# A two-layer transformer on one core: the modulation computed as visits of two k tiles, its columns read back through DRAM, and twenty of its parts placed outside the first MLP

## The chip, the cores and the metric

The kernel runs on one core of a Trainium2 chip. The metric is the device time of one execution in microseconds (us), as the median of several runs.

## The reference

Two transformer layers over 256 context and 512 latent tokens of width 1024: layer 0 with differential attention (8 heads), layer 1 with neighbourhood attention (16 heads, handled as 8 groups of two), each followed by a squared-ReLU MLP of width 4096. Both halves of a layer are modulated by vectors that depend on the conditioning inputs `c` (latent tokens) and `c_ctx` (context tokens) only:

```python
for i in range(DEPTH):
    mod_l = split(silu(c) @ w_mod[i] + b_mod[i], 6)        # w_mod[i] is 1024 x 6144
    mod_c = split(silu(c_ctx) @ w_mod[i] + b_mod[i], 6)
    x = x + mod_l[2] * mixer_i(rms_norm(x, norm1_g[i]) * (1 + mod_l[1]) + mod_l[0], ...)
    x = x + mod_l[5] * mlp(rms_norm(x, norm2_g[i]) * (1 + mod_l[4]) + mod_l[3])
    # the context tokens likewise with mod_c; after the last layer they are not needed
```

So per layer there are six sections of 1024 numbers for two streams: shift, scale and gate of the mixer (0, 1, 2) and of the MLP (3, 4, 5). All data is float32; most products are made of split operands in three passes.

## The kernel before, in words

The program runs in stages, each with its own partition of PSUM banks: a prologue with the first head (0 to 65 us), the first attention's heads (65 to 480), its out projection (to 544), the first MLP with its blend (to about 1115), the second attention's eight groups (to 1466), their projection, and the second MLP (from about 1506).

Activations lie transposed, model columns on the partitions. Shifts and scales are therefore wanted as columns: `mB` (shift) and `mA` ((1 + scale) times the norm's gain), 8 k tiles x 2 streams per section. The gates are wanted as rows and go to a DRAM tensor, `gates`, from which a broadcast load fetches them.

The modulation is cut in 48 chunks (`mod_chunk`, 24 a layer: six sections by four quarters of 256 columns). A chunk needs 1 MB of `w_mod`, loaded by SP into the tile M (L163), and does 8 matmuls in plain float32 (L263; 16 instructions in the trace), where the silu columns are the stationary operand and k tile kt writes to the 32 partitions of its quarter of the array, kt mod 4. The result in PSUM bank A is thus four partial sums on partitions 0, 32, 64 and 96 on. ScalarE copies them to a tile T (L266). A tail adds the four up with a matmul against the constant `sel`: for shift and scale as a column pair (L278, two matmuls of T's halves, then one or two small VectorE instructions, L285 to L289), for a gate as a row (L269, then a load of the bias, a VectorE add, L273, and a store, L274).

Where the chunks stand: eight (sections 0 and 1 of layer 0) in `first_head`; sixteen in the first attention; twenty-four, all of layer 1, in the first MLP, one at a call of `sideB`, which also steps the bias tables of the second attention.

The order of work around them: in both attentions PE, SP and POOL (`PINNED`) follow the order of the program, which the strings `START0`, `CYCLE0`, `END0`, `CYCLE1`, `LAST1`, `END1` write out by hand; `run` walks through a string. A word is a step: `Q0a` half a projection of the next head (L416), `S`, `T`, `V`, `U`, `O` the steps of the heads in flight (an apostrophe is an older head), `w` a weight load (SP, L130), `c` its split in a high and a low part, `x`, `X` loads and splits for the out projection, `P` a step of that; `m` begins a chunk and loads the next one's weights, `n` does its tail. In the second attention U is the transposition of normed queries and keys (L642 and L644 on PE, waiting for Y that VectorE makes in L431), T the transposition of the softmax's output (L695), V the sum over values (L710), which VectorE adds up in a tile T (L718). VectorE's and ScalarE's orders, and all orders in the MLPs, are the compiler's. The MLP's matmuls are L853 and L913, its last down part L994. `gated` in `project` (L766) multiplies by a gate row into a tile T.

## Time and profile before

| | |
|---|---|
| median of 3 runs | 1871.44 us (1870.74 to 1871.74) |
| profiled execution | 1864.46 us, span 1862.7 us |
| mean granted clock of TensorE | 0.983 |
| busy: PE, DVE, POOL, ACT | 1742.6, 1262.4, 1029.3, 948.0 us |
| DMA | 225.97 MB, of which 48 loads of 1 MB for the modulation |

PE is TensorE's matmuls, PEld its weight loads, DVE VectorE, ACT ScalarE, POOL GpSimd, SP the engine that issues most loads. A row of the timeline gives the start, the duration, the engine, the line, the operation with its output and inputs, and in brackets how long the engine was idle before it and what ended that. A matmul's end overlaps the next one's start, so what a piece of work holds of PE is read from start to start.

### The profile page before, as it was taken

To read this page: it belongs to the slowest core of one execution; us is meant where nothing else is said; L and a number is where in the kernel's file an instruction comes from. 1 tells how busy PE (TensorE), PEld (TensorE's weight loads), DVE (VectorE), ACT (ScalarE), POOL (GpSimd) and SP (SyncE) were. 2 spreads that over 40 slices of the span, in tenths; PEclk is the share of its full clock that TensorE was granted. 3 is DMA by queue.
4 is the path that set the end of the run, shared out by engine and by line. 5 is a ranking of instruction groups with operands and counts; after the bars stand their busy time and mean duration, and the time that the engine had idled before them with its cause. 6 is when DMAs were issued, how large, how long until landed. Compare 5 with 4: busy or idle time off the path is not lost.

```text
span 1862.7 us, 27761 instructions
## 1 busy us (share of the span) xinstructions
PE 1742.6 (94%) x10046; PEld 1523.8 (82%) x10046; DVE 1262.4 (68%) x2330; ACT 948.0 (51%) x2002; POOL 1029.3 (55%) x1002
## 2 busy tenths in 40 slices
PE   6989999996999999999999998999998989999988
PEld 5868888884789888888887987989897777878867
DVE  4587777786666465456466865777777557777785
ACT  4476667765344333233333345777776454445432
POOL 3755666653334555555555732444445547778873
PEclk9999999997999999999999998999999989999999
DMA  8122222224436646646643331122222424334432
GB/s 335 43 86 80 89 87 68 69 87 150 163 123 161 191 159 163 198 145 178 198 143 112 108 107 61 58 71 77 66 69 86 147 95 140 128 124 126 150 135 77
DMA packets 88554, 225.97 MB, mean 121 GB/s; under 512 B 9248, under 2 KB 24544, under 8 KB 82272
## 3 DMA queue, kind: packets, MB, share of 16 engines
q1 hardware_dynamic: 78928, 211.19, 35.0%
q10 hardware_dynamic: 9488, 13.00, 1.9%
q8 instruction: 79, 1.29, 0.3%
q14 instruction: 59, 0.48, 0.1%
HBM read 205.91 MB, written 18.25 MB: 120 GB/s over the span
## 4 chain that ended last, share of the span: by engine, by line
PE 66%; DVE 11%; ACT 7%; POOL 6%; issue 5%; DMA 4%; ACTq 0%; POOLq 0%; SPq 0%; DVEq 0%
PE PD L853 20%; PE PA L416 14%; PE PB L913 6%; PE PA L913 5%; POOL W L152 4%; PE PA L761 4%; PE PA L994 3%; PE PB L560 2%; PE PA L263 2%; DMA R<-in_w_dram 2%; PE PS L525 2%; PE PQ L406 1%; ACT W L146 1%; PE PS L664 1%; PE PB L710 1%
## 5 line engine op out<-in xcount | busy, mean ns | idle before, releaser
L152 POOL TENSOR_TENSOR W<-R,W 128x512 fp32r<-128x512 f32 x270 | 402.7, 1519 | 169.3 <-ACT W L146 163.5
L853 PE MATMUL PD<-Q,W 128*128 128x384 f32 (+2 forms) x1992 | 390.1, 346 | 9.2 <-DVE Q L340 5.6
L853 PEld LDWEIGHTS PD<-Q,W 128*128 128x128 f32 x1992 | 345.4, 189 | 40.4 <-issue 7.8
L146 ACT ACTIVATE W<-R 128x1024 fp32r<-128x1024 f32 (+1 forms) x165 | 168.1, 1022 | 195.6 <-DMA R<-in_w_dram 35.2
L152 POOL TENSOR_TENSOR W<-N,W 128x512 fp32r<-128x512 f32 x98 | 139.2, 1441 | 142.8 <-ACT W L146 142.4
L913 PE MATMUL PB<-W,H 128*128 128x512 f32 x738 | 190.8, 395 | 7.0 <-DVE Q L921 4.3
L913 PE MATMUL PA<-W,H 128*128 128x512 f32 x732 | 190.9, 396 | 4.5 <-DVE H L921 3.4
L416 PE MATMUL PA<-W,Q 128*128 128x384 f32 (+1 forms) x1008 | 175.8, 326 | 1.0 <-ACT H L454 1.0
L913 PEld LDWEIGHTS PB<-W,H 128*128 128x128 f32 x738 | 138.5, 189 | 39.5 <-DVE Q L921 5.2
L913 PEld LDWEIGHTS PA<-W,H 128*128 128x128 f32 x732 | 137.2, 190 | 37.2 <-DVE H L921 5.0
L302 POOL TENSOR_TENSOR SQ<-SQ,half 128x4 f32<-128x4 f32 (+1 forms) x96 | 93.8, 978 | 124.4 <-DVE SQ L429 123.5
L416 PEld LDWEIGHTS PA<-W,Q 128*128 128x128 f32 x1008 | 159.9, 192 | 1.2 <-ACT H L454 1.2
L146 ACT ACTIVATE W<-N 128x1024 fp32r<-128x1024 f32 x49 | 51.9, 1058 | 149.3 <-PE PA L913 66.4
L416 PE MATMUL PA<-WB,H 128*128 128x384 f32 x576 | 108.6, 340 | 0.8 <-DVE Q L477 0.8
L761 PE MATMUL PA<-W,H 128*128 128x512 f32 x384 | 97.6, 404 | 6.4 <-ACT H L752 4.4
L416 PEld LDWEIGHTS PA<-WB,H 128*128 128x128 f32 x576 | 98.7, 188 | 1.8 <-DVE Q L477 1.1
L871 DVE SCALAR_TENSOR_TENSOR H<-N,H 128x512 fp32r<-128x512 f32 (+1 forms) x57 | 70.8, 1244 | 41.9 <-ACT H L870 41.6
L853 PE MATMUL PD<-H,W 128*128 128x512 f32 (+1 forms) x408 | 94.7, 382 | 0.0
L761 PEld LDWEIGHTS PA<-W,H 128*128 128x128 f32 x384 | 72.3, 194 | 24.4 <-ACT H L752 4.8
L531 ACT ACTIVATE E<-PS,SA 128x768 f32<-128x768 f32 (+1 forms) x96 | 72.9, 760 | 35.2 <-DVE SA L530 31.6
L530 DVE TENSOR_REDUCE SA<-PS 128x1 f32<-128x768 f32 (+1 forms) x96 | 74.5, 776 | 20.8 <-ACT E L531 11.5
L676 POOL TENSOR_SCALAR E<-E,SA 128x256 f32<-128x256 f32 x64 | 59.5, 940 | 52.2 <-DVE SA L673 51.5
(258 smaller groups left out, 3564.0 us busy)
## 6 DMA issues: line engine op xcount, KB each, us to landing
R<-in_w_dram SPq DMA_DIRECT2D x121, 512.0 KB
M<-in_wmod_dram SPq DMA_DIRECT2D x48, 1024.0 KB
N<-in_w_dram SPq DMA_DIRECT2D x49, 512.0 KB
R<-in_wqa_dram SPq DMA_DIRECT2D x32, 384.0 KB
R<-in_wqb_dram SPq DMA_DIRECT2D x32, 384.0 KB
Y<-in_rpb_dram SPq DMA_DIRECT2D x48, 128.0 KB
bias<-Y SPq DMA_DIRECT2D x48, 128.0 KB
X<-bias SPq DMA_DIRECT2D x8, 768.0 KB
```

The source lines that it names most:

```text
L146: high = nc.scalar.activation(w[:, 0, :n], raw, AF.Copy)
L152: low = (eng or nc.gpsimd).tensor_sub(w[:, 1, o:e], raw[:, o:e], w[:, 0, o:e].bitcast(F32))
L302: nc.gpsimd.tensor_tensor(r, ss, self.half[:, :n], op=ALU.pow)
L416: nc.tensor.matmul(acc[:, :n], hT[kt][:, x, P * i:P * i + P], w[kt // 2][:, y, o:o + n], start=(kt == 0 and p == 0), stop=(kt == KT - 1 an ...
L530: nc.vector.tensor_reduce(mx, s, op=ALU.max, axis=AX, negate=True)
L531: nc.scalar.activation(e[:, m, :nk], s, AF.Exp, bias=mx[:, 0:1], accum_out=sm[:, m:m + 1])
L676: nc.gpsimd.tensor_scalar_mul(e[:, 1, o:o + 256], e[:, 1, o:o + 256], r[:, 1:2])
L761: nc.tensor.matmul(ps, oHL[h][:, x, c:c + P], w[h // 2][:, y, 512 * (h % 2):512 * (h % 2) + 512], start=(first and h == hs[0] and p == 0), ...
L853: nc.tensor.matmul(ps[:, at:at + b1 - b0], w[kt // 4][:, x, o:o + P], hT[kt][:, y, b0:b1], start=(kt == 0 and p == 0), stop=(kt == KT - 1 ...
L871: nc.vector.scalar_tensor_tensor(u[:, 1], src, 1.0, u[:, 0].bitcast(F32), op0=ALU.mult, op1=ALU.subtract)
L913: nc.tensor.matmul(ps, u[:, x, f, P * i:P * i + P], w[:, y, 512 * f:512 * f + 512], start=(f == 0 and p == 0), stop=(f == 1 and p == 2))
L994: nc.tensor.matmul(ps, hd[:, x, P * i - c0:P * i - c0 + P], w[f][:, y, 512 * n:512 * n + 512], start=(f == 0 and p == 0), stop=(f == len(h ...
```

## The change

A section of 1024 columns is now computed in four visits of two k tiles each (`mod_visit`), for all its four quarters: quarter q's partial sums go to partitions 32 q on. A visit has as many matmuls of the same shape as a chunk had. VectorE adds the visit's PSUM result to an accumulator tile MA (128x256), which a load has filled with the bias (`b_mod` on the two used rows of each quarter). After the fourth visit ScalarE's queue stores the four quarters' rows to a DRAM tensor `rows`; gates are later read from there as before from `gates`. For shifts and scales SP reads the rows back as columns ahead of the next visit, two DMAs of 128x8 single elements (one a stream), and one VectorE instruction makes `mB` or `mA` of all eight k tiles (`mod_set`). The copy by ScalarE, the column pairs and the row matmuls are gone, except in the first eight chunks, which stay as they were but for the place of the bias add.

The other forty chunks are now forty visits, in other places. Twenty (layer 0's sections 2 to 5 and layer 1's section 0) stand in the first attention, which had sixteen: five in START0, ten in the cycles, five in END0, where n is a visit that uses bank C. Four (layer 1's section 1) stay in the first MLP. Sixteen (layer 1's sections 2 to 5, `late`) stand in the second attention, two a group, their weights loaded as two halves of 512 KB into the tile C4 (the mask's) and a new pool M. The tag T has one buffer instead of two, and MA has two.

In the first MLP, PE's order before. The names are: PD, PA, PB the banks, Q and H activations, W weights; `x6` counts equal rows.

```order
L853 MATMUL PD_7522<-Q_6285,W_7467 128x384 x3
L853 MATMUL PD_7522<-Q_6286,W_7467 128x384 x3
L263 MATMUL PA_7573<-M_7448,silu 32x256 x8
L913 MATMUL PA_7613<-W_7605,H_7609 128x512 x6
L913 MATMUL PB_7622<-W_7605,H_7609 128x512 x6
L913 MATMUL PB_7648<-W_7641,H_7645 128x512 x6
L853 MATMUL PD_7714<-Q_6279,W_7704 128x384 x3
L853 MATMUL PD_7714<-Q_6280,W_7704 128x384 x3
L853 MATMUL PD_7714<-Q_6281,W_7704 128x384 x3
L278 MATMUL PA_7573<-sel,T_7582 128x2 x2
L853 MATMUL PD_7714<-Q_6282,W_7704 128x384
L913 MATMUL PA_7631<-W_7605,H_7609 128x512 x6
```

And at the same place in the changed kernel, behind its four visits:

```order
L851 MATMUL PD_7520<-Q_6293,W_7465 128x384 x3
L851 MATMUL PD_7520<-Q_6294,W_7465 128x384 x3
L911 MATMUL PA_7597<-W_7589,H_7593 128x512 x6
L911 MATMUL PB_7606<-W_7589,H_7593 128x512 x6
L911 MATMUL PA_7615<-W_7589,H_7593 128x512 x6
L911 MATMUL PB_7632<-W_7625,H_7629 128x512 x6
L851 MATMUL PD_7680<-Q_6287,W_7670 128x384 x3
L851 MATMUL PD_7680<-Q_6288,W_7670 128x384 x3
L851 MATMUL PD_7680<-Q_6289,W_7670 128x384 x2
L911 MATMUL PA_7641<-W_7625,H_7629 128x512 x6
L851 MATMUL PD_7680<-Q_6289,W_7670 128x384
L851 MATMUL PD_7680<-Q_6290,W_7670 128x384 x2
```

The chunk (L263) and its column pair (L278) are gone from between the MLP's matmuls (L853 and L913, now L851 and L911), whose own order has shifted a little.

In the second attention, PE before, from a half of the query projection (L416) to the transposition of queries and keys (L642, L644) at U4':

```order
L416 MATMUL PA_12265<-W_12053,Q_6716 128x256 x3
L416 MATMUL PA_12265<-W_12053,Q_6717 128x256 x3
L695 MATMUL PB_12280<-ident,E_12096 128x128 x4
L695 MATMUL PB_12287<-ident,E_12096 128x128 x4
L642 MATMUL PA_12294<-ident,Y_12164 128x128
L644 MATMUL PA_12294<-ident,Y_12164 128x128
```

And in the changed kernel (L416, L695, L642, L644 are now L414, L693, L640, L642):

```order
L414 MATMUL PA_11988<-W_11756,Q_6724 128x256 x3
L414 MATMUL PA_11988<-W_11756,Q_6725 128x256 x3
L289 MATMUL PA_12001<-C_11896,silu 32x256 x4
L289 MATMUL PA_12001<-M_11897,silu 32x256 x4
L693 MATMUL PB_12017<-ident,E_11799 128x128 x4
L693 MATMUL PB_12024<-ident,E_11799 128x128 x4
L640 MATMUL PA_12031<-ident,Y_11867 128x128
L642 MATMUL PA_12031<-ident,Y_11867 128x128
```

A visit (L289), four matmuls on each half of its weights, has come in ahead of L693. The second visit of a group stands likewise ahead of the L640 of U2.

On SP in the changed kernel, where a section has just been completed in the second attention (MA the bias, C and M the halves of a visit's weights, R weights of a later group, SA the columns read back, X a bias table):

```order
L1051 DMA MA_14054<-in_bmod_dram 128x256
L163 DMA C_14056<-in_wmod_dram 128x1024
L163 DMA M_14057<-in_wmod_dram 128x1024
L130 DMA R_14144<-in_wqb_dram 128x768
L130 DMA R_14146<-in_wqb_dram 128x768
L1060 DMA SA_14161<-rows 128x8x1 x2
L163 DMA C_14175<-in_wmod_dram 128x1024
L163 DMA M_14176<-in_wmod_dram 128x1024
L130 DMA R_14233<-in_wqb_dram 128x768
L130 DMA R_14465<-in_wqb_dram 128x768
L635 DMA X_14549<-bias 128x1536
```

And VectorE there (L291 the add of a visit, L279 the column set, L695 the eviction of the transposed softmax, before L697, L716 the sum over values, before L718, L429 the norm's product, before L431):

```order
L427 TENSOR_REDUCE SQ_14121<-sq_83 128x4
L451 TENSOR_TENSOR H_14002<-PA_14060,H_14001 64x256
L716 TENSOR_TENSOR T_13996<-PB_14131,T_13996 64x256
L291 TENSOR_TENSOR MA_14054<-PA_14165,MA_14054 128x256
L451 TENSOR_TENSOR H_14002<-PA_14060,H_14001 64x256
L695 TENSOR_TENSOR N_14179<-PB_14181,N_14179 128x512
L279 SCALAR_TENSOR_TENSOR mA<-SA_14161,gT 128x16
L695 TENSOR_TENSOR N_14180<-PB_14188,N_14180 128x512
L429 SCALAR_TENSOR_TENSOR Y_14118<-Y_14118,SQ_14123 128x256
```

The reads stand behind the next visit's two halves and two weights; the column set stands behind the next visit's add and between the two evictions of one T step.

The diff, cut: left out are the removed lines of `mod_chunk` and `Mods` (they stand in the listing above), the loads of `w_mod` by a shared helper `mod_raw` (SP, one 1 MB load or two halves), and the tables' new layouts.

```diff
--- before.py
+++ after.py
@@ -35,19 +35,19 @@
-CYCLE0 = """w0 w1 Q0a O2'' n1' S1' O3'' V4'' V5'' c0 w2 U4' Q0b c1 w3 Q1a T0' T1' Q1b c2 O4'' S2' V0' Q2a O5'' Q2b
-S3' T2' U0 Q3a V1' c3 O0' Q3b S4' T3' Q4a Q4b V2' O1' m0 S5' T4' U2 n0 Q5a V3' Q5b m1 S0 T5'"""
-START0 = """w0' w1' Q0a' Q0b' Q1a' U0'' Q1b' c0' w2' Q2a' Q2b' U2'' c1' w3' Q3a' Q3b' S0'' U4'' c2' Q4a' S1'' m0 c3'
-T0'' Q4b' S2'' V0'' n0 T1'' V1'' S3'' T2'' U0' Q5a' Q5b' m2 O0'' S4'' T3'' n2 w0 w1 Q0a U2' O1'' V2''
-S5'' T4'' Q0b c0 w2 V3'' S0' Q1a O2'' V4'' U4' Q1b c1 w3 O3'' T5'' m3 O4'' S1' T0' V5'' c2 V0' n3 S2' T1'
-Q2a O5'' Q2b S3' V1' c3 O0' U0 Q3a T2' Q3b Q4a S4' T3' Q4b V2' Q5a T4' S5' O1' V3' Q5b S0 T5' m1 U2"""
-END0 = """x0 x1 x2 x3 S1' O2'' O3'' V4'' T0' U4' n1' X0 V5'' T1' X1 S2' O4'' X2 x4 V0' S3' x5 P0a O5'' T2' X3 P1a
-X4 V1' O0' S4' X5 B0 P0b m0 V2' O1' x6 P1b T3' n0 P2a T4' S5' P2b O2' P3a V3' V4' P3b m1 T5' P4a O3' n1
+CYCLE0 = """w0 w1 Q0a O2'' S1' O3'' V4'' V5'' c0 w2 U4' Q0b c1 w3 Q1a T0' T1' Q1b c2 O4'' S2' V0' Q2a O5'' Q2b
+S3' T2' U0 Q3a V1' c3 O0' Q3b S4' T3' Q4a Q4b V2' O1' m S5' T4' U2 Q5a V3' Q5b m S0 T5'"""
+START0 = """w0' w1' Q0a' Q0b' Q1a' U0'' Q1b' m c0' w2' Q2a' Q2b' U2'' c1' w3' Q3a' Q3b' S0'' U4'' c2' Q4a' S1'' m c3'
+T0'' Q4b' S2'' V0'' T1'' V1'' S3'' T2'' U0' Q5a' Q5b' m O0'' S4'' T3'' w0 w1 Q0a U2' O1'' V2''
+S5'' T4'' Q0b c0 w2 V3'' S0' Q1a O2'' V4'' U4' Q1b c1 w3 O3'' T5'' m O4'' S1' T0' V5'' c2 V0' S2' T1'
+Q2a O5'' Q2b S3' V1' c3 O0' U0 Q3a T2' Q3b Q4a S4' T3' Q4b V2' Q5a T4' S5' O1' V3' Q5b S0 T5' m U2"""
+END0 = """x0 x1 x2 x3 m S1' O2'' O3'' V4'' T0' U4' X0 V5'' T1' X1 m S2' O4'' X2 x4 V0' n S3' x5 P0a O5'' T2' X3 P1a
+X4 V1' O0' n S4' X5 B0 P0b V2' O1' x6 P1b T3' P2a T4' S5' P2b O2' P3a V3' V4' m P3b T5' P4a O3'
 X6 P4b V5' P5a P5b O4' O5'"""
-CYCLE1 = """w0 w1 Q0a T3'' U4' Q1a c0 w2 V2'' V3'' Q0b S0' Q1b Q2a S1' Q2b Q3a T0' S2' Q4a c1 w3 T1' Q3b S3' V0' U0
-Q4b c2 U2 Q5a T2' Q5b c3 V1'"""
-LAST1 = """Q0a T3'' U4' Q1a c0 x0 x1 V2'' V3'' Q0b S0' Q1b X0 x2 Q2a S1' Q2b X1 Q3a T0' S2' Q4a T1' Q3b X2 S3' V0'
-U0 Q4b U2 Q5a T2' Q5b V1'"""
+CYCLE1 = """w0 w1 Q0a m T3'' U4' Q1a c0 w2 V2'' V3'' Q0b S0' Q1b Q2a S1' Q2b Q3a T0' S2' Q4a c1 w3 T1' Q3b S3' V0' U0
+Q4b c2 m U2 Q5a T2' Q5b c3 V1'"""
+LAST1 = """Q0a m T3'' U4' Q1a c0 x0 x1 V2'' V3'' Q0b S0' Q1b X0 x2 Q2a S1' Q2b X1 Q3a T0' S2' Q4a T1' Q3b X2 S3' V0'
+U0 Q4b m U2 Q5a T2' Q5b V1'"""
 END1 = """x3 x4 T3'' c1 U4' V2'' V3'' S0' X3 x5 P2a S1' c2 X4 P3a T0' S2' X5 T1' P4a B0 S3' V0' V1' P2b T2' x6 P3b
...
@@ -76,7 +76,7 @@
         self.room, self.turns, self.last = {"R": [(self.rpool, 2, None)]}, {}, {}
-    BUFS = {"H": 8, "Q": 8, "E": 2, "X": 2, "Y": 6, "T": 2, "SQ": 12, "SA": 12, "SO": 8, "C4": 1}
+    BUFS = {"H": 8, "Q": 8, "E": 2, "X": 2, "Y": 6, "T": 1, "MA": 2, "SQ": 12, "SA": 12, "SO": 8, "C4": 1}
...
@@ -262,34 +258,37 @@
             q = kt % 4
             nc.tensor.matmul(ps[32 * q:32 * q + 32, 0:256], self.silu[:, kt, :], raws[kt],
                              start=kt < 4, stop=kt >= 4)
...
+        sb = self.sbt('Y', [P, 256])
         nc.scalar.activation(sb, ps[:, 0:256], AF.Copy)
...
         for b in range(2):
             nc.tensor.matmul(ps[:, 256 + 2 * b:256 + 2 * b + 2], sb[:, P * b:P * b + P], self.sel[:, 0:2],
                              start=True, stop=True)
+        ks = slice(2 * qtr, 2 * qtr + 2)
+        t = self.sbt('SQ', [P, 2, 2])
+        nc.vector.tensor_add(t, ps[:, 256:260].rearrange("p (k s) -> p k s", s=2),
+                             self.bT[:, sec, ks, None].to_broadcast([P, 2, 2]))
+        self.mod_set(0, sec, ks, t)
+
+    def mod_set(self, l, sec, ks, t):
+
         norm = sec // 3
...
         if sec % 3 == 0:
...
+            self.nc.vector.tensor_copy(self.mB[:, l, norm, ks, :], t)
         else:
...
+            n = ks.stop - ks.start
+            self.nc.vector.scalar_tensor_tensor(
+                self.mA[:, l, norm, ks, :], t, 1.0, self.gT[:, norm, l, ks, None].to_broadcast([P, n, 2]),
                 op0=ALU.add, op1=ALU.mult)
...
+
+    def mod_visit(self, acc, v, raws, bank):
+
+        nc = self.nc
+        ps = self.pst(bank)
+        for k in range(2):
+            for q in range(4):
+                nc.tensor.matmul(ps[32 * q:32 * q + 32, 0:256], self.silu[:, 2 * v + k, :], raws[4 * k + q],
+                                 start=k == 0, stop=k == 1)
+        nc.vector.tensor_add(acc, ps[:, 0:256], acc)
     def rstd(self, ss, n, tag):
...
@@ -1038,26 +1036,39 @@
 class Mods:
...
+    def __init__(self, b, todo, halves=()):
+        self.b, self.halves, self.ready, self.back = b, halves, [], []
+        self.todo = [(l, sec, v) for l, sec in todo for v in range(4)]
+        self.acc = None
+
+    def load(self):
+        b = self.b
+        if not self.todo:
+            return
+        l, sec, v = self.todo.pop(0)
+        if v == 0:
+            self.acc = b.sbt('MA', [P, 256])
+            b.nc.sync.dma_start(self.acc, b.a["bmod"][l, sec])
+        self.ready.append((l, sec, v, self.acc, b.mod_raw(b.a["wmod"][l, sec, v], self.halves)))
+
+    def visit(self, bank='A'):
+
+        b, nc = self.b, self.b.nc
+        for l, sec in self.back:
+            t = b.sbt('SA', [P, KT, 2])
+            for s in range(2):
+                nc.sync.dma_start(t[:, :, s], b.rows[l, sec, s].rearrange("(k p) -> p k", p=P))
+            b.mod_set(l, sec, slice(0, KT), t)
+        self.back = []
         if self.ready:
...
+            l, sec, v, acc, raws = self.ready.pop(0)
+            b.mod_visit(acc, v, raws, bank)
+            if v == 3:
+                for q in range(4):
+                    nc.scalar.dma_start(b.rows[l, sec, :, 256 * q:256 * q + 256], acc[32 * q:32 * q + 2])
+                if sec in (0, 1, 3, 4):
+                    self.back.append((l, sec))
+        self.load()
 def run(order, c, steps, load, split, **others):
...
@@ -1081,20 +1092,20 @@
         b = Block(tc, ctx, a)
         xs = a["xin"].rearrange("(t p) d -> t p d", p=P)
-        first = [(0, 4 * s + q) for q in range(4) for s in (0, 1)]
-        mods = Mods(b, first + [(0, n) for n in range(8, 24)] + [(1, n) for n in range(24)])
+        mods = Mods(b, [(0, 2), (0, 3), (0, 4), (0, 5), (1, 0), (1, 1)])
+        late = Mods(b, [(1, 2), (1, 3), (1, 4), (1, 5)], ("C4", "M"))
         done = []
-        mod = {"m": lambda _: (mods.begin(), mods.load(True)), "n": lambda _: mods.end()}
+        mod = {"m": lambda _: mods.visit('A'), "n": lambda _: mods.visit('C')}
         b.open("left", WA=4)
             xnT = b.normed_early(xs)
-            hT, accs = b.first_head(xnT, mods)
+            hT, accs = b.first_head(xnT)
             b.setup_layer0(*tabs)
             b.open("right", M=1, O=4, OT=2, WB=4)
-            mods.load(True)
+            mods.load()
             heads = {0: b.head0(0, accs=accs)}
...
@@ -1144,8 +1155,7 @@
             units, begun = [b.bias1(u) for u in range(6 * GROUPS1)], []
             def sideB():
-                mods.chunk()
-                mods.load(True)
+                mods.visit()
...
@@ -1163,6 +1173,8 @@
         b.close("W", "N", "OT", "O", "M", "W")
         b.open("right", VM=2, N=4, W1=2)
+        b.open("left", M=1)
+        late.load()
         with b.psum_phase("psC", **PS_ATTN1):
...
@@ -1179,7 +1191,7 @@
             with tc.manual_schedule(engines=PINNED):
                        "x": lambda n: proj["fetch"](int(n)),
-                       "X": lambda n: proj["split"](int(n), nc.gpsimd)}
+                       "X": lambda n: proj["split"](int(n), nc.gpsimd), "m": lambda _: late.visit()}
                 for c in range(GROUPS1):
...
@@ -1187,7 +1199,7 @@
                         proj.update(b.project(1, a["wob"], b.oT1, 2, lambda i: b.x2[i - 2], 'HQ', 'QH', 'S1', done))
                     run(CYCLE1 if c < GROUPS1 - 1 else LAST1, c, heads, load, split, **own)
-                b.close("W1")
+                b.close("M", "W1")
                 b.open("left", W=3)
```

More of the change, by code (lines that the diff above doesn't have):

```diff
@@ L156, in wsplit, with mod_raw @@
         return w
[L158 to L169 removed]
+    def mod_raw(self, src, halves=()):
+        ws = [self.sbt(t, [P, 1024]) for t in halves] or [self.sbt('M', [P, 2048])]
+        o = 0
+        for w in ws:
+            self.nc.sync.dma_start(w, src[:, o:o + w.shape[1]])
+            o += w.shape[1]
+        return [w[:, o:o + 256] for w in ws for o in range(0, w.shape[1], 256)]
     def setup(self):
@@ L203, in setup @@
         self.mB = c.tile([P, 2, 2, KT, 2], F32, name="mB")
-        self.gates = self.dram.tile([2, 2, 2, D], F32, name="gates")
+        self.rows = self.dram.tile([2, 6, 2, D], F32, name="rows")
     def load_layer0(self):
@@ L731, in load_gates @@
             g = self.sbt('N', [P, D])
-            self.nc.sync.dma_start(g, self.gates[l, which, s:s + 1, :].to_broadcast([P, D]))
+            self.nc.sync.dma_start(g, self.rows[l, 3 * which + 2, s:s + 1, :].to_broadcast([P, D]))
             out[s] = g
@@ L1146, in sideB @@
             def sideB():
-                mods.chunk()
-                mods.load(True)
+                mods.visit()
                 for u in begun:
```

68 lines of the change are left out of this document (13 added, 55 removed).

## The prediction

> **What bounds the kernel now.** I read first the page's busy time and its chain of waits.
>
> ```profile
> PE 1742.6 (94%) x10046; PEld 1523.8 (82%) x10046; DVE 1262.4 (68%) x2330; ACT 948.0 (51%) x2002; POOL 1029.3 (55%) x1002
> PE 66%; DVE 11%; ACT 7%; POOL 6%; issue 5%; DMA 4%; ACTq 0%; POOLq 0%; SPq 0%; DVEq 0%
> ```
>
> TensorE sets the time, but not everywhere, so I then asked for busy time by stretch: the first attention's heads (65 to 480), the inside of the first MLP (600 to 1000), its end with the border to the second attention, the second attention's groups (1130 to 1440), and its end. Columns: busy us of PE, PEld, DVE, ACT, POOL, then granted clock, DMA share, GB/s.
>
> ```profile
> 65.00:480.00 415.00, 376.17 (x2440) 335.22 (x2441) 317.09 (x745) 275.09 (x785) 235.44 (x318) 0.97 0.25 88
> 600.00:1000.00 400.00, 397.74 (x2255) 341.87 (x2254) 217.87 (x287) 138.34 (x171) 224.80 (x170) 1.00 0.57 174
> 1000.00:1130.00 130.00, 120.61 (x617) 106.11 (x616) 100.88 (x173) 54.43 (x93) 67.06 (x52) 0.98 0.24 78
> 1130.00:1440.00 310.00, 282.60 (x1928) 274.08 (x1927) 228.29 (x526) 214.97 (x531) 134.74 (x182) 0.97 0.21 70
> ```
>
> Inside the first MLP PE idles 2.3 us of 400 and no other engine exceeds 56%: one us of PE work there is one us of time. In the second attention PE idles 27.4 us of 310, in the first 38.8 of 415; work put there costs nothing if it meets the idle time. Then I asked what PE waits for in the second attention (waited for: total us, times, longest).
>
> ```profile
> PE PA L642 <- DVE Y L431: 16.6, 16, 3.2
> PE PB L695 <- DVE T L718: 8.1, 7, 1.4
> ```
>
> These two make up 24.7 of the 27.4 us, twice or thrice in each group.
>
> **The price of a visit.** The modulation's matmuls inside the MLP, by line (L263 the matmuls of a chunk, 16 records each; L278 the column pair; L269 the gate row), and two chunks in PE's timeline, the last two rows from the first attention:
>
> ```profile
> 600.00:1000.00 400.00, 24.62 (x368) 9.60 (x368) 1.00 0.57 174
> 600.00:1000.00 400.00, 7.53 (x60) 8.85 (x60) 1.00 0.57 174
> 600.00:1000.00 400.00, 4.95 (x16) 1.10 (x16) 1.00 0.57 174
> ```
>
> ```profile
> 854.30 1.07 PE L263 MATMUL PA<-M,silu 128*32 128x256 f32 x16
> 855.31 4.14 PE L853 MATMUL PD<-Q,W 128*128 128x384 f32 x22
> 859.29 0.50 PE L278 MATMUL PA<-sel,T 128*128 128x2 f32 x4
> 859.65 6.05 PE L853 MATMUL PD<-Q,W 128*128 128x384 f32 x33
> ...
> 413.77 0.62 PE L269 MATMUL PA<-T,sel 128*32 128x256 f32 x2
> 414.32 2.35 PE L416 MATMUL PA<-WB,H 128*128 128x384 f32 x12
> ```
>
> The busy times overlap their neighbours, so I go from start to start: a chunk holds PE for 855.31 - 854.30 = 1.01 us, a column pair 0.36, a gate row 0.55. A visit issues as many matmuls of the same shape as a chunk, so 1.01 us; its new VectorE add (128x256, PSUM plus SBUF) I take from the row of that form, 0.43 us, and with it goes ScalarE's copy:
>
> ```profile
> L667 DVE TENSOR_TENSOR PS<-PS,X x64: 418/432/433, 1156.9 to 1446.8; 128x256 f32<-128x256 f32 x64
> L266 ACT ACTIVATE T<-PA x48: 362/384/400, 26.6 to 994.0; 128x256 f32<-128x256 f32 x48
> L273 DVE TENSOR_TENSOR T<-PA,T x16: 402/405/413, 99.2 to 998.6; 2x256 f32<-2x256 f32 x16
> ```
>
> **First MLP.** Of 24 chunks (16 with a column pair, 8 with a gate row) 4 visits stay. PE is rid of 20 x 1.01 + 16 x 0.36 + 8 x 0.55 = 20.2 + 5.8 + 4.4 = 30.4 us. With the 20 go their 1 MB loads and copies, which no one waited for. Four adds of 0.43 us and two column sets go to a DVE with 182 us free. The compiler chooses the order in this stage, and the 2.3 us of idle may change; the work taken away can't save more than itself, so 24 to 31, and I take **-29.5**.
>
> **First attention.** It had 16 chunks and gets 20 visits: +4 x 1.01 = +4.0. Eight column pairs and eight gate rows go: -8 x 0.36 - 8 x 0.55 = -7.3, where PE was waiting anyway nothing; as PE idles 9% here, I count -5 (-7.3 to -3). DVE gets 20 x 0.43 = 8.6 us and loses 8 x 0.41 = 3.3 and some 2 of small adds: +3.3 on 317 busy of 415, counted +0.5 (0 to +3). The last part, the tail of the heads, is the delicate place (SP's timeline, stretches, PE's timeline with the idle time and its releaser in brackets):
>
> ```profile
> 411.21 10.37 SPq L163 DMA_DIRECT2D M<-in_wmod_dram  x2
> ```
>
> ```profile
> 411.20:413.20 2.00, 2.00 (x14) 1.77 (x15) 0.91 (x4) 0.85 (x4) 1.92 (x3) 1.00 0.63 149
> 413.20:415.20 2.00, 2.00 (x13) 1.42 (x12) 2.00 (x5) 1.92 (x5) 1.37 (x3) 1.00 1.00 401
> 415.20:417.20 2.00, 2.00 (x15) 2.00 (x14) 1.74 (x4) 1.20 (x3) 1.87 (x3) 1.00 0.10 41
> ...
> 425.00:450.00 25.00, 17.75 (x69) 13.81 (x70) 15.29 (x36) 13.59 (x36) 8.73 (x11) 0.66 0.50 187
> ```
>
> ```profile
> 425.71 1.22 PE L525 MATMUL PS<-Q,Q 128*128 128x256 f32 x4 [3.19 <-ACT E L531]
> ...
> 462.28 0.73 PE L761 MATMUL PA<-W,H 128*128 128x512 f32 x2 [4.39 <-ACT H L752]
> ...
> 1129.35 9.36 PE L416 MATMUL PA<-H,Q 128*128 128x384 f32 x36 [3.64 <-DVE H L629]
> ```
>
> A 1 MB load issued at 411.21 has landed about 415.6 (149 then 401 GB/s, and 41 after): 4.4 us. The tail's first visit is now right behind the last cycle's and ahead of L525 at 425.71; its load starts at about 421.2 and lands at 425.6, so L525 starts about 1 us later. The other four find PE idle 7 us in 425 to 450. On SP four M loads of 4.4 us now stand ahead of the projection's later loads of head outputs, and PE already waits 4.39 us for the split of one (L752, above); the first four stay ahead of the visits, so I count nothing beyond the 1 us (0 to +6: the later splits as much later as a load and a half).
> Together +4.0 - 5 + 0.5 + 1 = **+0.5** (-4 to +8). By the Trainium skill, TensorE: Matmul & The Clock Gate, Part 1 on the clock gate, an idle window of about 3.4 us halves the clock; the 0.66 behind the 3.19 us wait agrees. By that rule visits that break up the waits would keep the clock up and be worth up to 17.75 x 0.34 = 6 us, an estimate; but the first can't start before 425.6, so I add nothing.
>
> **Second attention.** 16 visits, 16.2 us of PE, two a group: one ahead of the second L695 pair, one ahead of L642. In the group at 1205 to 1244:
>
> ```profile
> 1217.96 0.33 PE L642 MATMUL PA<-ident,Y 128*128 128x128 f32 x1 [1.27 <-DVE Y L431]
> ...
> 1227.58 0.66 PE L695 MATMUL PB<-ident,E 128*128 128x128 f32 x4 [1.07 <-DVE T L718]
> ...
> 1228.90 0.33 PE L642 MATMUL PA<-ident,Y 128*128 128x128 f32 x1 [0.45 <-DVE Y L431]
> ```
>
> Waits of 1.27 and 1.07 us stand exactly where a visit of 1.01 goes, so its matmuls cost nothing as long as they don't delay the chain that ends the wait. Its add does: behind the first visit it stands in DVE's queue ahead of the L431 that ends the 0.45 us wait, so each group gets about 0.43 us, 8 x 0.43 = 3.4. A third bank-A tile is taken and released by the add; the last and the first group's waits differ. The bounds: all hidden, 0; none hidden, 16.2 + 16 x 0.43 = +23. It is nearest to the waits shown, and I take **+4**. The 1 MB loads, 4.4 us each, have about 10 us from the second visit (L642, 1217.96) to the next first one (1227).
>
> **Reading back.** Four sections are turned into columns while pinned orders run (two in each attention): an add, four ScalarE stores, two SP reads of 128x8 single elements, and one DVE instruction that waits for them in order, as the DVE order shows, with the L695 evictions that PE waits for behind it. No run here has such a read. From below: 128 packets, nothing. From above: 1024 packets each. The page's queue rows price a packet:
>
> ```profile
> q1 hardware_dynamic: 78928, 211.19, 35.0%
> q10 hardware_dynamic: 9488, 13.00, 1.9%
> ```
>
> q10: 0.019 x 16 x 1862.7 / 9488 = 60 ns; q1: 132 ns, with 2.7 KB in each. At 60, two reads take 2 x 1024 / 16 x 0.060 = 7.7 us. In the second attention they follow, on SP, 1 MB of M halves and two 384 KB weights (4.4 us at 400 GB/s); with 1 us of stores they land about 13 us after the add; DVE gets there after 10 (m to m) to 12. Say 2 us of stall, a third of it felt by PE: 4 x 0.6 = **+2.5** (0 to +10). By the Trainium skill, DMA: Bandwidth & Descriptors, Rules for kernel authors, a non-contiguous last dim lowers to one descriptor per element: its rule speaks against this change and is the upper end just worked out.
>
> **Border, end and prologue.** The first late visit's second half lands only after the last down matmuls; PE waited 3.64 us there before the Q projections (the L629 row above), which may cover it: +1 (0 to +3). One T buffer instead of two at the second projection, whose gated sums (L766) use the tag: 0 (0 to +3). The first head gains a small DVE op in four chunks: +0.5 (0 to 1).
>
> **Sum**: -29.5 + 0.5 + 4 + 2.5 + 1 + 0.5 = -21.0 us against the profiled execution's 1864.5 (span 1862.7 and 1.8 around it), 1843.5. The median of the runs is 1871.4, 7 us above that execution; on it, the forecast is **1850.4**.
>
> **Rivals.** *The second attention hides little.* If each visit shifts the chain too (bank A late, the add ahead of other evictions), half of 23 more than I counted is lost: +16 instead of +4, 1862. For it: DVE is 74% busy there, and it is DVE that both waits are for. Against: both waits are longer than a visit.
> *Something else paces the MLP.* The gain shrinks to about half, 1865. Only POOL (56%) could; against it, the 2.3 us of idle.
> *The reads come late: slower.* One mechanism: DVE stands at the column set, the evictions and L431 behind it wait, PE with them, four times. It costs 4 x (reads + 5.4 - 11), and outweighs the 23.5 us of all else when a stall passes 5.9 us, that is when two reads take over 11.5 us, 90 ns a packet. At q1's 132 ns they take 16.9: 4 x 11.3 = 45 - 23.5, +21.7, 1893. For it: each packet carries 4 bytes, a form none of these queues shows; against: q10 does smaller ones (1.4 KB) at 60.
> *The tail of the first attention* starves: +6, 1856. That the work isn't moved is excluded by the order: four visits in the MLP, sixteen later.
>
> **Chances.** Forecast 0.58 (1842 to 1857), second attention 0.19, MLP 0.05, tail 0.07, reads 0.11. All but the reads are faster; what a measurement can tell is 0.2%, 3.7 us, and at the edges of the second and third rivals lie 0.04 for same. Faster 0.86, same 0.04, slower 0.10. The range, 1839 to 1868, leaves out the reads and a little on either side.
>
> **What would show it.** Right: in the changed profile the stage from the MLP's first to last matmul is about 29 us shorter with PE still at 99%; the groups of the second attention are 39 to 40 us apart; waits for L431 and L718 have shrunk by about 13 us; the column sets begin on DVE within 2 us of the instruction before. Wrong: an idle DVE ahead of the four sets, PE idle behind the second attention's visits for M or C, or an MLP with new waits.

## The result, and the profile after

The changed kernel takes 1849.74 us as the median of four runs (1847.18 to 1851.53), the kernel before 1871.09; the ratio is 0.9894, with a 95% interval of 0.9877 to 0.9910. By the ratio it is 20 us faster, 3 either way; the medians differ by 21.4. Forecast were 1850.4 us, in a range of 1839 to 1868. So the total came as predicted; its parts did not, as the stages show. The page of the changed kernel, busy time and chain:

```profile
PE 1729.0 (93%) x9918; PEld 1521.2 (82%) x9918; DVE 1265.9 (68%) x2328; ACT 936.8 (51%) x1962; POOL 1046.2 (57%) x1002
PE 65%; DVE 11%; ACT 7%; POOL 6%; issue 5%; DMA 5%; ACTq 0%; SPq 0%; POOLq 0%; DVEq 0%
```

PE is still what sets the end, with 13.6 us less work. To see where the time went, both programs are cut at the same matmuls. In the following rows (start and end, length, then busy time by engine, clock, DMA share and GB/s) the stages are: first score of the first attention to the MLP; first L913 to the first last-down matmul; last of these to the first score of the second attention; first to last score there; from there to the second MLP; the second MLP. The kernel before:

```profile
87.10:544.30 457.20, 421.26 (x2649) 368.54 (x2649) 339.48 (x779) 287.11 (x801) 238.13 (x317) 0.97 0.28 97
586.20:1073.90 487.70, 481.66 (x2672) 418.03 (x2671) 288.19 (x372) 170.55 (x207) 285.55 (x213) 1.00 0.52 157
1113.60:1156.20 42.60, 33.97 (x196) 32.44 (x195) 24.22 (x66) 20.26 (x53) 9.45 (x15) 0.88 0.19 63
1156.20:1446.40 290.20, 265.84 (x1846) 256.94 (x1845) 221.05 (x509) 209.58 (x513) 128.50 (x171) 0.99 0.21 71
1446.40:1496.60 50.20, 47.17 (x237) 38.66 (x236) 29.14 (x54) 22.36 (x45) 30.24 (x28) 1.00 0.40 131
1496.60:1862.70 366.10, 345.77 (x1521) 281.51 (x1519) 262.45 (x317) 157.68 (x215) 255.06 (x171) 0.97 0.37 124
```

The changed kernel (1849.7 us of span):

```profile
86.80:543.70 456.90, 419.56 (x2650) 368.31 (x2650) 341.98 (x781) 281.82 (x785) 238.38 (x317) 0.97 0.31 105
585.50:1032.10 446.60, 442.88 (x2276) 403.10 (x2276) 281.37 (x345) 165.33 (x184) 300.13 (x213) 1.00 0.45 125
1072.20:1119.50 47.30, 38.93 (x244) 35.50 (x243) 24.80 (x70) 20.04 (x52) 9.44 (x15) 0.86 0.39 128
1119.50:1425.50 306.00, 285.31 (x2054) 266.16 (x2053) 226.21 (x525) 211.09 (x516) 128.16 (x171) 0.97 0.33 110
1425.50:1479.60 54.10, 48.83 (x236) 39.74 (x235) 30.26 (x53) 21.54 (x43) 29.30 (x28) 0.97 0.38 123
1479.60:1849.70 370.10, 347.31 (x1521) 281.59 (x1519) 260.38 (x317) 157.54 (x215) 256.56 (x171) 0.97 0.36 122
```

The inside of the first MLP is 41.1 us shorter, where 29.5 were forecast; the first attention is the same (-0.3); the border +4.7, the second attention +15.8 and its end +3.9 give 24.4 us back, where 7.5 were forecast (4, 1 and the 2.5 of the reads). Two errors, of 12 and some 17 us, stand against each other; that they cancel is luck. These two executions differ by 13.0 us only, since the one of the kernel before lies at the low end of its runs and this one at the high end; second profiles of both (below) differ by 21.5. The last row differs by 4.0 us though its code is the same; the last runs bear on that.

What PE waits for in the second attention (1119.5 to 1412.2) has changed its kind. The waits for L716 (L718 before), seven of them, are gone but for one, and of the waits for L429 (L431) the longest is now 4.5 us:

```profile
PE PA L640 <- DVE Y L429: 14.2, 7, 4.5
PE PB L693 <- DVE T L716: 1.7, 1, 1.7
```

The timeline of VectorE at the longest of them, in the group whose first visit follows a completed section:

```profile
1234.18 0.69 DVE L695 TENSOR_TENSOR N<-PB,N 128x512 fp32r<-128x512 f32 x1 [0.30 <-ACT N L694]
1237.53 0.17 DVE L276 COPY mB<-SA 128x16 f32<-128x16 f32 x1 [2.66 <-DMA SA<-rows]
1237.61 0.68 DVE L695 TENSOR_TENSOR N<-PB,N 128x512 fp32r<-128x512 f32 x1
1238.21 0.41 DVE L429 SCALAR_TENSOR_TENSOR Y<-Y,SQ 128x256 f32<-128x256 f32 x1
```

VectorE stands 2.66 us at the column set, and what PE needs (the second L695, L429) is behind it. SP and PE there:

```profile
1227.24 4.91 SPq L130 DMA_DIRECT2D R<-in_wqb_dram  x2
1232.37 1.00 SPq L1060 DMA_DIRECT2D SA<-rows  x2
```

```profile
1238.68 0.47 PE L640 MATMUL PA<-ident,Y 128*128 128x128 f32 x1 [4.51 <-DVE Y L429]
...
1239.02 2.91 PE L414 MATMUL PA<-W,Q 128*128 128x256 f32 x12
...
1245.36 1.65 PE L414 MATMUL PA<-W,Q 128*128 128x256 f32 x12
```

The reads were issued only when SP had got past two weight loads, at 1232.37, and VectorE went on 5.2 us later. And behind PE's wait of 4.51 us the same twelve matmuls take 2.91 us instead of 1.65: the granted clock has dropped.

```profile
1240.00:1245.00 5.00, 5.00 (x27) 5.00 (x26) 1.85 (x5) 1.60 (x4) 0.00 (x0) 0.53 0.01 6
1245.00:1250.00 5.00, 5.00 (x43) 5.00 (x42) 3.49 (x9) 3.19 (x10) 0.00 (x0) 1.00 0.14 52
```

The granted clock is 0.53 for these 5 us and 1.00 after. By the Trainium skill (TensorE: Matmul & The Clock Gate, Part 1 on the clock gate) an idle window of about 3.4 us does that; this trace agrees. In the same profile the clock is also 0.50 from 978.5 to 981.5, behind a wait of 2.56 us, which is shorter than that window. So from the second visit of the group before (1222.1) to that of this one (1267.9) it takes 45.8 us; where nothing disturbs, 39.0 (1183.1 to 1222.1).

### The profile page after: what moved, and what is told of

The parts are those of the page before. It is cut to its first block, busy times and chain, and to the rows that moved or that the text cites. A ratio compares the mean times of both kernels' runs of the same rounds, so it can differ in the third digit from the quotient of the medians.

```text
span 1849.7 us, 27540 instructions
## 1 busy us (share of the span) xinstructions
PE 1729.0 (93%) x9918; PEld 1521.2 (82%) x9918; DVE 1265.9 (68%) x2328; ACT 936.8 (51%) x1962; POOL 1046.2 (57%) x1002
## 2 busy tenths in 40 slices
DMA packets 104809, 227.29 MB, mean 123 GB/s; under 512 B 22160, under 2 KB 38752, under 8 KB 100576
## 4 chain that ended last, share of the span: by engine, by line
PE 65%; DVE 11%; ACT 7%; POOL 6%; issue 5%; DMA 5%; ACTq 0%; SPq 0%; POOLq 0%; DVEq 0%
PE PD L851 19%; PE PA L414 14%; PE PB L911 6%; PE PA L911 6%; PE PA L759 4%; POOL W L152 4%; PE PA L992 3%; DMA R<-in_w_dram 3%; PE PS L523 2%; PE PB L558 2%; PE PQ L404 1%; ACT W L146 1%; PE PS L662 1%; PE PB L708 1%; PE PB L693 1%
## 5 line engine op out<-in xcount | busy, mean ns | idle before, releaser
L152 POOL TENSOR_TENSOR W<-R,W 128x512 fp32r<-128x512 f32 x270 | 416.3, 1570 | 162.2 <-ACT W L146 161.4
L851 PE MATMUL PD<-Q,W 128*128 128x384 f32 (+2 forms) x1992 | 379.8, 344 | 11.7 <-DVE Q L339 5.6
L851 PEld LDWEIGHTS PD<-Q,W 128*128 128x128 f32 x1992 | 345.6, 189 | 35.0 <-ACT W L146 7.6
L911 PE MATMUL PB<-W,H 128*128 128x512 f32 x738 | 191.9, 395 | 5.5 <-DVE Q L919 4.4
L911 PE MATMUL PA<-W,H 128*128 128x512 f32 x732 | 190.9, 395 | 3.8 <-DVE H L919 2.6
L414 PE MATMUL PA<-W,Q 128*128 128x384 f32 (+1 forms) x1008 | 175.8, 327 | 0.0
L911 PEld LDWEIGHTS PB<-W,H 128*128 128x128 f32 x738 | 139.5, 190 | 36.0 <-DVE Q L919 5.2
L301 POOL TENSOR_TENSOR SQ<-SQ,half 128x4 f32<-128x4 f32 (+1 forms) x96 | 95.3, 994 | 128.3 <-DVE SQ L427 127.1
L911 PEld LDWEIGHTS PA<-W,H 128*128 128x128 f32 x732 | 137.9, 189 | 34.6 <-DVE H L919 3.0
L414 PEld LDWEIGHTS PA<-W,Q 128*128 128x128 f32 x1008 | 159.9, 193 | 0.9
L414 PE MATMUL PA<-WB,H 128*128 128x384 f32 x576 | 108.7, 342 | 2.6 <-DVE Q L475 2.6
L414 PEld LDWEIGHTS PA<-WB,H 128*128 128x128 f32 x576 | 98.7, 189 | 3.5 <-DVE Q L475 3.4
L851 PE MATMUL PD<-H,W 128*128 128x512 f32 (+1 forms) x408 | 95.2, 383 | 0.0
L529 ACT ACTIVATE E<-PS,SA 128x768 f32<-128x768 f32 (+1 forms) x96 | 72.9, 759 | 40.4 <-DVE SA L528 36.9
```

Of the source, the lines that this page charges most:

```text
L152: low = (eng or nc.gpsimd).tensor_sub(w[:, 1, o:e], raw[:, o:e], w[:, 0, o:e].bitcast(F32))
L301: nc.gpsimd.tensor_tensor(r, ss, self.half[:, :n], op=ALU.pow)
L414: nc.tensor.matmul(acc[:, :n], hT[kt][:, x, P * i:P * i + P], w[kt // 2][:, y, o:o + n], start=(kt == 0 and p == 0), stop=(kt == KT - 1 an ...
L529: nc.scalar.activation(e[:, m, :nk], s, AF.Exp, bias=mx[:, 0:1], accum_out=sm[:, m:m + 1])
L851: nc.tensor.matmul(ps[:, at:at + b1 - b0], w[kt // 4][:, x, o:o + P], hT[kt][:, y, b0:b1], start=(kt == 0 and p == 0), stop=(kt == KT - 1 ...
L911: nc.tensor.matmul(ps, u[:, x, f, P * i:P * i + P], w[:, y, 512 * f:512 * f + 512], start=(f == 0 and p == 0), stop=(f == 1 and p == 2))
```

## The experiments

The theory was that the MLP gained more than the visits' own time because every break in its matmuls costs something beside, and that the second attention hides the visits but not the column sets. The rivals: the MLP gained from the loads that left; the second attention is slowed by the visits themselves.

**All late visits back in the first MLP.** Form without place.

```diff
-mods = Mods(b, [(0, 2), (0, 3), (0, 4), (0, 5), (1, 0), (1, 1)])
-late = Mods(b, [(1, 2), (1, 3), (1, 4), (1, 5)], ("C4", "M"))
+mods = Mods(b, [(0, 2), (0, 3), (0, 4), (0, 5)] + [(1, n) for n in range(6)])
 # no m in CYCLE1 and LAST1, no pool M there
```

> The sixteen late visits go back into the first MLP (twenty there), in the new form; the second attention has none. It separates the form of the change from the place. Theory: in the profile of the changed kernel the first MLP is 41 us shorter though my prices explain 30; each break in the MLP's matmuls costs some 0.2 us beyond the 1.01 us of a visit, and the second attention lost about 11 us to two waits for read-back columns, the rest to its first and last groups. Then the first MLP grows by 16 x (1.01 + 0.2) = 19 us against the changed kernel, the second attention with its border and projection returns to what it was before (-20 to -25 us), and the total is -6 to 0 us against the changed kernel. Rival: the MLP gained because 20 MB of loads left, whatever the matmuls did; then the first MLP grows by 24 us or more and the total is 0 to +5 us.

Measured: ratio 0.9904 (0.9889 to 0.9918), 1849.46 us: no slower than the changed kernel by what can be told. Its inside of the MLP and its second attention, first to last score:

```profile
584.50:1051.10 466.60, 462.87 (x2532) 408.72 (x2532) 292.44 (x363) 165.18 (x184) 294.26 (x213) 1.00 0.53 156
1132.30:1421.30 289.00, 264.65 (x1847) 256.09 (x1846) 221.78 (x510) 209.73 (x513) 127.73 (x171) 0.99 0.21 71
```

Sixteen visits cost the MLP 20.0 us, 1.25 each, of which 1.00 is the visit from start to start; the rest is in the MLP's own matmuls (L851 and L911), which took 444.0 us from start to start against 440.1 in the changed kernel. The second attention is back at 289.0. So the new form with all of layer 1's visits but four in the MLP is worth what the whole change is: moving sixteen of them out gained 20.0 us there and lost 17.0 in the second attention and 5.9 at its border.

**The loads alone.** Sixteen loads of 1 MB in the first MLP that nothing uses.

```diff
 def sideB():
     mods.visit()
+    calls.append(0)
+    if 5 <= len(calls) <= 20:
+        i = len(calls) - 5
+        b.mod_raw(a["wmod"][1, 2 + i // 4, i % 4])
```

> The changed kernel with sixteen more loads of 1 MB into M in the first MLP, which nothing uses: the loads of the moved chunks without their matmuls. It tells what of the MLP's 41 us came from the loads. Theory: PE never waited for them, so the first MLP stays at 488 us, within 2. Rival: writes of loads slow PE's reads or delay the weights; then the MLP grows by 4 to 10 us, which would be the part of the 41 us that my prices don't explain.

Measured: ratio 0.9953 (0.9937 to 0.9970); the MLP's inside took 455.0 us, 8.4 more than the 446.6 of the changed kernel (the expectation's 488 is the stage of the kernel before). That is the rival's size and the second half of its mechanism, the weights delayed, but in one place only, by a wait of PE that no other run has, and one of VectorE ahead of it (687 to 700 us):

```profile
PE PA L911 <- DVE E L919: 6.0, 1, 6.0
DVE N L927 <- DMA N<-in_w_dram: 9.0, 1, 9.0
```

```profile
678.01 12.62 SPq L163 DMA_DIRECT2D M<-in_wmod_dram  x3
690.74 0.89 SPq L890 DMA_DIRECT2D N<-in_w_dram  x2
```

Three loads into M, each of which waits for the one before it, hold up SP for 12.6 us ahead of the weights N (L890); VectorE waits for these, and PE for VectorE. In this stage SP waits 49.3 us for a load of M before the next, in the kernel before 9.8, and there no such wait reaches PE; so this run doesn't show that the chunks' loads cost anything. The MLP's own matmuls took 442.5 us, 2.4 more than in the changed kernel, and 2.3 of that lie right behind the wait, from 700.4 to 705.0 us, where the granted clock is 0.50. So what the loads cost here is that one stall. At first the 2.4 looked like a part of the 4.0 above, so it was also tested the other way.

**The visits without loads.** Sixteen more visits in the first MLP that multiply the last real visit's weights again and add into a spare tile (work that the reference does not need).

```diff
+    if 5 <= len(calls) <= 20:
+        b.mod_visit(spare, (len(calls) - 5) % 4, mods.kept, 'A')
```

> The changed kernel with sixteen more visits in the first MLP that load nothing: they multiply the weights of the last real visit again and add into a tile that nothing uses. With the run that has the loads alone (the MLP's own matmuls took 2.4 us more) and the one that has both (+20.0 us: 16.0 the visits, 4.0 the MLP's own matmuls, from start to start) it tells what slows the MLP's matmuls. If the loads do, the MLP's own matmuls take about 440 to 441 us here as in the changed kernel (L851 236, L911 204) and the stage grows by 16 us. If the breaks do, they take 442 to 444 us and the stage grows by 18 to 20 us.

Measured, in one execution: the MLP's inside took 466.6 us, +20.0, with 444.0 us for its own matmuls, both the same as with the loads. The breaks do it, 0.25 us each, and the loads add nothing to that. The starts of the single matmuls in both traces show where: the last one ahead of a visit takes 0.09 us longer to the next start than its like (0.268 us against 0.175 for L851), and the first one behind a visit 0.11 us longer, together 0.20 of the 0.25. The kernel before fits: 449.0 us for its own matmuls, with 46 breaks (23 chunks, 15 column pairs, 8 gate rows in that stretch), against 440.1 with three: 8.9 us over 43 breaks, 0.21 each.

**The column set one visit later.**

```diff
-            b.mod_set(l, sec, slice(0, KT), t)      # with the reads
+            reads.append((l, sec, t))
 ...
+    def set(self):                                   # behind the next visit's add
+        for l, sec, t in self.read:
+            self.b.tc.keep_in_program_order(self.b.mod_set(l, sec, slice(0, KT), t))
```

> The instruction on VectorE that uses the columns read back (L276, L279) comes one visit later than the reads and stays behind that visit's add; nothing else changes. Theory: in the second attention VectorE stood 2.66 and 1.23 us at these instructions, and the two groups in which it did took 45.8 and 43.3 us against 39.0 in the undisturbed ones. Without the waits these groups take 39 to 40 us, the second attention is 10 us shorter, the first 1 to 2 us; total -8 to -12 us against the changed kernel. Rival: the long groups have another cause (the late loads of M and C, weights that SP issues late); then they stay above 42 us and the total moves by less than 3 us.

Measured: ratio 0.9877 (0.9862 to 0.9891). VectorE no longer stands at a column set; first to last score took 299.0 us instead of 306.0, its end 52.6 instead of 54.1, the first attention 455.5 instead of 456.9. That is 9.9 us in these stages, of which the ratio shows about 3, with intervals of 3 us to either side on two chips; the 8 to 12 us of the expectation did not come. The waits were the cause of 7 us in the second attention (5.6 against the changed kernel's second profile, below), less than the 10 expected: the two long groups took 40.4 and 42.1 us instead of 45.8 and 43.3. What was left was seen in the same trace: the groups behind a completed section still waited 2.12 us for L429, the others 0.45. VectorE and POOL in such a group:

```profile
1231.84 0.42 DVE L427 TENSOR_REDUCE SQ<-sq 128x4 f32<-128x260 f32 x1
1232.17 0.41 DVE L451 TENSOR_TENSOR H<-PA,H 64x256 fp32r<-64x256 f32 x1
1232.61 0.43 DVE L716 TENSOR_TENSOR T<-PB,T 64x256 f32<-64x256 f32 x1
1233.08 0.42 DVE L291 TENSOR_TENSOR MA<-PA,MA 128x256 f32<-128x256 f32 x1
1233.53 0.43 DVE L451 TENSOR_TENSOR H<-PA,H 64x256 fp32r<-64x256 f32 x1
...
1235.90 0.42 DVE L429 SCALAR_TENSOR_TENSOR Y<-Y,SQ 128x256 f32<-128x256 f32 x1
```

```profile
1234.02 0.40 POOL L456 CAST H<-H 64x256 fp32r<-64x256 f32 x1 [0.92 <-DVE H L451]
1234.50 1.01 POOL L301 TENSOR_TENSOR SQ<-SQ,half 128x4 f32<-128x4 f32 x1
```

The sum of squares (L427) is ready at 1232.3, but POOL's power (L301) starts at 1234.50, behind a cast that waits for the second L451, and this L451 stands behind the visit's add. In the other groups the compiler has put the work differently: in the next one the sum of squares is ready at 1273.4 and POOL's power starts at 1273.59. One of the three long waits follows a gate's section, which is not read back as columns, so it isn't the reads that do it.

**SP stores the rows.** The four stores of a section go from ScalarE's queue to SP's, one visit later, with reads and set following.

```diff
-                for q in range(4):
-                    nc.scalar.dma_start(b.rows[l, sec, :, 256 * q:256 * q + 256], acc[32 * q:32 * q + 2])
+                self.full.append((l, sec, acc))     # nc.sync.dma_start at the next visit's begin
```

> As the run with the columns set a visit later, but SP stores a section's rows, at the next visit, and ScalarE issues none (except for the last section); reads and column sets follow one visit later each. Theory: in that run the groups behind a completed section still waited 2.12 us for L429 where the others waited 0.45, because in those groups the compiler, which counts the four store issues on ScalarE, puts the add (L291) and a sum (L451) ahead of the norm's product (L429), and POOL's queue has a cast that waits for that sum ahead of the power that the product needs. With the stores on SP all groups have the order of the undisturbed ones: waits of 0.45 us in all, three groups 1.7 us shorter, the second attention 5 us shorter than in that run (first score to last: 299 to 294 us). Rival: the wait comes with the first visit of a section itself (its bias load); then three waits of about 2 us stay and the attention is within 1 us of 299.

Measured: ratio 0.9821 (0.9796 to 0.9845), 1833.63 us. From the second group to the seventh PE waits 0.45 us at L429, in each, and first to last score takes 292.5 us. VectorE and PE in the group that took 45.8 us in the changed kernel:

```profile
1224.91 0.42 DVE L427 TENSOR_REDUCE SQ<-sq 128x4 f32<-128x260 f32 x1
1225.36 0.43 DVE L716 TENSOR_TENSOR T<-PB,T 64x256 f32<-64x256 f32 x1
1225.82 0.42 DVE L291 TENSOR_TENSOR MA<-PA,MA 128x256 f32<-128x256 f32 x1
1226.51 0.59 DVE L429 SCALAR_TENSOR_TENSOR Y<-Y,SQ 128x256 f32<-128x256 f32 x1 [0.27 <-POOL SQ L301]
```

```profile
1224.21 0.64 PE L289 MATMUL PA<-C,silu 128*32 128x256 f32 x8
1224.67 0.61 PE L289 MATMUL PA<-M,silu 128*32 128x256 f32 x8
1225.22 1.28 PE L693 MATMUL PB<-ident,E 128*128 128x128 f32 x8
...
1227.16 0.33 PE L640 MATMUL PA<-ident,Y 128*128 128x128 f32 x1 [0.45 <-DVE Y L429]
```

The wait is the one of the kernel before, and a visit stands in the place of the L716 wait. From first to last score the visits now cost 2.3 us over the kernel before, and 1.9 at the border. What is shown is that with the stores on SP, one visit later, the compiler makes another order, and that the order before it cost the time. Whether the queue or the later place does it was not separated, and that it is the stores' issue time in the compiler's model was inferred and not tried.

**Two T buffers at the end.**

```diff
-                b.open("left", W=3)
+                b.open("left", W=3, T=2)
```

> Two buffers of the tile T from the end of the second attention on, as before the change; it has one otherwise. Theory: PE waited 2.6 us once for a gated sum of the second projection (L759 for DVE T L764), which no wait of the kernel before answers; this goes, and the second projection's end comes 2 to 3 us earlier, total -2 to -3 us. Rival: the sums are late because the last group's value sums are late on VectorE, and the wait only changes its place: 0 us.

Measured: ratio 0.9902 (0.9887 to 0.9917), no gain that can be told. PE's wait for L764 (2.6 us) is gone and the stretch to the second MLP took 50.6 us instead of 54.1; the total didn't follow. In all profiles with one T buffer, the one without late visits among them (54.4), this stretch took 52.6 to 55.3 us, with two buffers 50.2 to 52.2.

**Everything together**, with two visits moved in the first attention's tail:

```diff
-END0 = """x0 x1 x2 x3 m S1' O2'' ... V0' n S3' x5 ...
+END0 = """x0 x1 x2 x3 S1' m O2'' ... V0' S3' n x5 ...
```

> The run with SP's stores, and besides two T buffers at the second projection and, in the tail of the first attention, the first visit moved behind S1' and the fourth part's visit behind S3', where its load has landed. Theory: each stage gives its own part: second attention 294 us from first to last score, end of the second attention to the second MLP 50.5 instead of 54 us, tail of the first attention 3 to 5 us shorter (PE waited 3.8 and 1.5 us for M there); total 16 to 20 us below the changed kernel. Rival: the tail is bound by ScalarE's chain (L529, L750), and its end moves by less than 1 us; then 12 to 15 us.

Measured: ratio 0.9829 (0.9806 to 0.9853), 1834.77 us, not better than the version with SP's stores without these two, and 15.2 us below the changed kernel where 16 to 20 were forecast. The tail shows why: the wait for M shrank and others grew in its place (401 to 545 us, first this version without, then with the two moves).

```profile
PE PA L289 <- DMA M<-in_wmod_dram: 5.9, 2, 4.7
PE PC L289 <- DMA M<-in_wmod_dram: 1.9, 1, 1.9
PE PS L523 <- ACT E L529: 1.0, 1, 1.0
```

```profile
PE PS L523 <- ACT E L529: 7.0, 2, 4.3
PE PA L289 <- DMA M<-in_wmod_dram: 2.4, 2, 2.2
```

The stage took 455.5 us with them and 455.4 without. Here, and at the second projection (52.2 us against 52.6), the rival held: the wait changes its place.

**Both kernels again.**

> The changed kernel once more, beside the others on the same chip, as their base: ratio 0.989 to the kernel before; stages within 1 us of its first profile, where the second MLP took 3.6 us longer than in the profile of the kernel before, of the same code. If that is the execution and not the kernel, the second MLP here is anywhere between 339 and 344 us.

> The kernel before once more, for a second profile: its first, 1864.5 us, lies at the low end of its runs. If the second MLP (first matmul to its last down part, 339.0 us in the first profile) takes 342 to 344 us here, as in all profiles of the changed form, the 3.6 us are no effect of the change; if it is 339 again, they are, though the code is the same. The first MLP should take 487 to 489 us between its first L913 and its first L994.

Measured, on the chip of the two faster versions: the changed kernel 1849.96 us, ratio 0.9908 (0.9890 to 0.9926), so the version with SP's stores is 16 us faster than it. Of the kernel before this is one execution. Stages of the second profiles: the MLP's inside 446.6 and 487.0 us as before within 0.7; second attention 304.6 and 290.0; its end 55.3 and 52.0. The second MLP, from its first matmul to its last down part, took 339.2 us in the changed kernel here and 342.6 in its first profile, 339.0 and 339.1 in the kernel before, and between 340.7 and 345.1 in the other runs. As one program does both, its difference isn't put down to the change; why the kernel before showed the low value twice stays open.

## Why the prediction was right, and where not

The total was right, and its likeliest case, but by two mis-sized terms of opposite sign; that they cancel to within 1 us is luck. Of the signs that it named, groups 39 to 40 us apart came only where no section had just been completed; an idle VectorE ahead of the column sets, a sign of being wrong, came too, and so did PE's wait for a late visit's M (1.78 us, at the border).

- **First MLP, -29.5; it was -41.1.** The prices of what was removed held: chunks and tails took 32.9 us from start to start in the kernel before and 3.0 after, 29.9 against the 30.4 of the sum. What failed is the sentence that "the work taken away can't save more than itself": every break also slows the MLP's own matmuls, 8.9 us in all, and 2.3 us of idle time went too. Start to start of the inserted rows is not the whole price of inserting them.
- **First attention, +0.5; it was -0.3.** The first visit of the tail did wait for its load, 3.79 us rather than one, and others 0.48 and 1.52; the tail's other waits (401 to 545 us) shrank by more, from 17.7 to 9.9 us, as the two moved visits showed from the other side.
- **Second attention, +4.** The mechanism, visits in the place of waits, was right: in the version without the later disturbances the groups are 39.0 us apart, 39.1 before, and thirteen visits cost 2.3 us between the first and the last score; the first three stand ahead of it, where that version is 1.9 us longer, so 4.2 in all. The add's 0.43 us a group wasn't lost; L429 comes 0.45 us late with and without it.
- **Reading back, +2.5.** The place was right, the four column sets, and so was the end from which it came: one packet per element. The page counts 22160 packets under 512 bytes, where it had 9248; the 12912 more are the twelve reads' 12288 and some.

```profile
DMA packets 88554, 225.97 MB, mean 121 GB/s; under 512 B 9248, under 2 KB 24544, under 8 KB 82272
DMA packets 104809, 227.29 MB, mean 123 GB/s; under 512 B 22160, under 2 KB 38752, under 8 KB 100576
```

  So the rule of the Trainium skill (DMA: Bandwidth & Descriptors, Rules for kernel authors), a descriptor per element of a non-contiguous last dim, agrees. But a packet is cheap: VectorE went on 3.5 to 5.2 us after the first issue of two reads, so that 2048 packets on 16 engines, as the prediction counts them, took 41 ns each at most (5.2 x 16 / 2048), an estimate, not 60 or 132. That is why the slower rival, which needed 90, didn't come. The stalls were near the 2 us forecast (2.66, 1.23, 1.21 and 0.28 us), but "a third of it felt by PE" was the step that failed: 3.9 us of stall in the second attention cost 7.0 (5.6 against the second profile), as VectorE's evictions behind it all came late and one wait, 4.5 us long, also lowered the clock. And the term missed what came with the four stores on ScalarE at the end of a section: the compiler's order of three groups was worse, and with the stores on SP a visit later the second attention is 6.5 us shorter.
- **Border, +1; it was +4.7.** Two visits and the second half of the first stand there, 2.6 us, which the term left out. The first did wait 1.78 us for M, but PE's idle time there is 8.4 us in all, 8.6 before. The rest is the query projection (L414), 31.6 us from start to start against 29.4. **T, 0**: the stretch with the second projection takes 52.6 to 55.3 us with one buffer and 50.2 to 52.2 with two, so the term was some 2 us; in the total two buffers showed nothing. **Prologue, +0.5**: -0.3.
- **The rivals.** Something else pacing the MLP: no, PE is busy 442.9 of 446.6 us. The second attention hiding little: its size came (+15.8), its reason didn't, since bank A ended one wait only (0.8 us).

## What to carry to other kernels

The price of small work between an engine's long rows is the stage with it minus the stage without it, not the width of its own rows; here a quarter more. An instruction that nobody needs soon but that waits for a long chain (store, load, semaphore) should be put where the chain has long ended, in each in-order queue that it passes: moving VectorE's wait and ScalarE's stores made the second attention 12.1 us shorter on the same chip, of the 16 us that the better version gains. And a sum that comes out right is checked by stage before its terms are used again.

## What the runs showed that was not expected

Breaks of 1 us in PE's stream cost the matmuls around them 0.21 to 0.25 us, with granted clock 1.00, with loads and without; 0.20 of that lies in the one matmul ahead of the break and the one behind it. Behind a wait of 4.51 us on PE the granted clock was 0.53 from 1240 to 1245 us, so that, with 0.45 us of it the usual wait, the group was 6.8 us longer. Column reads of single elements, two at a time with 1024 packets each, had landed when VectorE went on, 3.5 to 5.2 us after their first issue.
